# Attention scores as pairs of 64-row matmuls on the two row halves, in periods of three key-tile pairs, with the recurrence's level rounds beside probability-value batches

## The chip, the cores and the metric

One core of a Trainium2 chip. The time is that of one launch of the whole layer in device microseconds, lower is better; the median of three runs is given. TensorE (PE, with its weight loads PEld), VectorE (DVE), ScalarE (ACT) and GpSimd (POOL) work in parallel, each in the order of its own queue, and wait for one another by semaphores. SyncE (SP) issues the DMAs.

## The reference, cut to what matters

One layer of a hybrid backbone over 2048 latent and 256 context tokens, width 1024, all in 32-bit floats: a combined projection, grouped-query attention (8 query heads on 2 key heads, head size 64) beside a gated linear recurrence in both directions (4 heads of 128), an output projection and a feed-forward part. The change is in the attention; the recurrence runs between.

```python
def latent_attention(qx, kx, vx, kc, vc):
    keys = jnp.concatenate([kc, kx], axis=1)          # 2304 keys
    vals = jnp.concatenate([vc, vx], axis=1)
    scale = ATT_HEAD_DIM ** -0.5
    def block(q):                                     # 128 queries
        s = jnp.einsum('bqkgd,bnkd->bkgqn', q, keys).astype(jnp.float32) * scale
        p = jax.nn.softmax(s, axis=-1)
        return jnp.einsum('bkgqn,bnkd->bqkgd', p.astype(vals.dtype), vals)
```

## The kernel before

After the projections, one stage does attention and recurrence together. Attention is cut into 32 items: a key head `g` and 128 queries `qt` of its four query heads. Queries and keys are each split into a high and a low part, so that a product of two splits needs three terms (high by high, low by high, high by low).

For an item, `chunk` (nine of them, L910 to L943) first multiplies the high parts alone, queries by 512 keys at a time for two heads, and VectorE takes the minimum of the (negated) scores over the keys. The two matmuls of a chunk use 64 rows each, one on the upper half of the array's rows and one on the lower; they write the two banks of one PSUM tile `mx`, of which there is one. `maxima` (L945) transposes the four columns `neg` and copies them with four small DMAs into row 0 of the query tile `qb`. The chunks of item n+1 are made while item n has its scores.

`scores(k)` (L954) makes one tile of 128 keys by 512 queries with two matmuls of 128 rows: `KS` holds high and low keys one above the other and meets the high queries twice; `KB` holds a row of -1 (which subtracts the maximum), zeros and the high keys, and meets `qb` with the maxima in row 0 and the low queries below. Three PSUM tiles `s` go round. ScalarE turns each into probabilities with an exponential, two tiles to one buffer `p` (a pair). POOL adds two of three pairs (`ps`, L972). `products` (L974) multiplies six key tiles' probabilities by the values, in two column halves of 64 (`av`, L981), and sums them with a column of ones in 32-column pieces (L989). `finish` (L998) spreads the reciprocal (`pb`, L1002) and scales.

The recurrence, four heads of sixteen units in all, runs in rounds of two "lanes": a round's matmuls `pa` (L646) have 128 rows and 64 columns, and the `level` behind it works on all other engines. Other steps are `diagonal` (`pd`), `keys` (`pk`), `forward` (`psf`), `backward` (`psb`) and `output` (`po`), all with 128 rows and 128 columns. A unit's start copies on ScalarE and multiplies on POOL.

TensorE's order in this stage is written out by hand: 18 ticks to an item, one score tile to a tick; `CHUNKS` gives the ticks of the chunks, `LAGT` puts a batch of products three ticks behind its scores, and a round of the recurrence comes every ninth tick. So some rounds fall beside a batch and others between scores. The other engines' orders are the framework's, from the order in which the work is written.

Of the kernel before, what the change touches and what calls it, by code (L numbers as in the profile page):

```python
# [9 lines left out]
F32 = mybir.dt.float32  # L10
F32R = mybir.dt.float32r
# [57 lines left out]
def block_kernel(ctx: ExitStack, tc: tile.TileContext, a: dict, out: bass.AP, dbg=None):  # L69
# [141 lines left out]
    with ExitStack() as st:  # L211
# [217 lines left out]
        def qk_side(t, c):  # L429
# [55 lines left out]
            else:  # L485
# [11 lines left out]
                for g in range(2):  # L497
                    nc.sync.dma_start(s_k[g][:, t * P:(t + 1) * P], f32v(sf[:, g * P:(g + 1) * P]))
# [69 lines left out]
    with ExitStack() as st:  # L568
# [327 lines left out]
        BATCH = 6  # L896
        LAGT = 3

        class Item:
# [7 lines left out]
            def load(self):  # L907
                self.qa = qpl.tile([P, 512], F32R, tag="qa", name=f"qa{self.nm}", bufs=3)
                src = s_q[self.g][self.qt]
                for dup in range(2):  # L910
                    nc.sync.dma_start(f32v(self.qa[dup * 64:(dup + 1) * 64, :]),
                                      src[0].rearrange("d h x -> d (h x)"))

            def load_low(self):
                self.qb = QB[self.n % 2]
                nc.sync.dma_start(f32v(self.qb[64:, :]), s_q[self.g][self.qt, 1].rearrange("d h x -> d (h x)"))

            def chunk(self, c):

                if c == 0:  # L920
                    self.mn = sm.tile([P, 4, 5], F32, tag="mn", name=f"mn{self.nm}")
                s = ps_mx.tile([P, 2, 512], F32, tag="x", name=f"mx{self.nm}_{c}")
                if self.n in (NCH, NCH + 1):
                    sides = ((slice(0, P), KS[self.g]),) * 2
                else:
                    sides = ((slice(0, 64), KS[self.g]), (slice(64, P), KB))

                def part(o, h0, k0, n):
                    for i, (ps, K) in enumerate(sides):
                        nc.tensor.matmul(s[:, i, o:o + n], self.qa[ps, (h0 + i) * P:(h0 + i + 1) * P],  # L930
                                         K[ps, k0:k0 + n], start=True, stop=True)

                if c < 8:
                    h, k = c // 4 * 2, c % 4
                    part(0, h, k * 512, 512)
                    nc.vector.tensor_reduce(self.mn[:, h:h + 2, k], s, axis=AX.X, op=ALU.min)  # L936
                else:
                    for h in range(0, 4, 2):
                        part(h * 128, h, 2048, 256)
                    nc.vector.tensor_reduce(self.mn[:, :, 4].rearrange("p (h i) -> p i h", i=2),  # L940
                                            s.rearrange("p i (h k) -> p i h k", h=2), axis=AX.X, op=ALU.min)
# [3 lines left out]
            def maxima(self):  # L945

                pm = ps_h.tile([P, 512], F32, tag="h", name=f"pn{self.nm}")
# [3 lines left out]
                for h in range(4):  # L951
                    nc.sync.dma_start(f32v(self.qb[0:1, h * P:(h + 1) * P]), f32v(mr[h:h + 1, :]))

            def scores(self, k):  # L954

                nm = f"{self.nm}_{k}"
                p = k // 2
                if k % 2 == 0:
                    self.pairs[p] = pp.tile([P, 1024], F32, tag="p", name=f"p{self.nm}_{p}")
                s = ps_st.tile([P, 512], F32, tag="s", name=f"s{nm}")  # L960
                ks = slice(k * P, (k + 1) * P)
                nc.tensor.matmul(s, KS[self.g][:, ks], self.qa, start=True, stop=False)  # L962
                nc.tensor.matmul(s, KB[:, ks], self.qb, start=False, stop=True)  # L963
                o = k % 2 * 512
                nc.scalar.activation(self.pairs[p][:, o:o + 512], s, AF.Exp, scale=-1.0)  # L965
                if k % BATCH == 3:
                    self.add(p)
# [641 lines left out]
```

## Time and profile before

| what | us |
|---|---|
| median of 3 runs (3406.96 to 3409.92) | 3408.22 |
| the profiled execution's own time | 3398.26 |
| its span, first to last instruction | 3396.5 |
| stage with scores, first to last (L962) | 755.8 to 1839.2 |
| items in the stage | 32 |

The profiled execution is a little faster than the median of the runs; durations come from it. In a row of the timeline stand start, length, engine, line, operation, output and inputs with their shape, and in brackets how long the engine was idle ahead and who released it. A matmul's length includes its way through the array; the distance between two starts tells what it costs in a stream. A group's row gives count, busy time, mean in ns and idle time ahead.

### The profile page before, as it was taken

What the parts mean: (1) busy time and instruction counts of PE and PEld (TensorE: products, weight loads), DVE (VectorE), ACT (ScalarE), POOL (GpSimd) and SP (SyncE); (2) the same over time, 40 slices, a digit from 0 to 9 for tenths busy, and PEclk for the clock granted to TensorE, in tenths of its full rate; (3) what the DMA queues carried; (4) which work ended last, traced back from release to release, by engine and by line L of the source; (5) the groups of instructions that cost most, each with busy time, mean ns of one, the idle gap of its engine ahead of it and who ended that gap; (6) DMA issues with size and microseconds to landing.
All of it is one profiled execution on the core that took longest, in us unless ns stands there. A gap on an engine that the chain in (4) does not pass through costs nothing. (4 is left out here: it accounts for less than half of the span.)

```text
span 3396.5 us, 55490 instructions
## 1 busy us (share of the span) xinstructions
PE 3235.6 (95%) x21212; PEld 2514.5 (74%) x21212; DVE 1725.5 (51%) x2742; ACT 1303.6 (38%) x2559; POOL 1636.5 (48%) x1450
## 2 busy tenths in 40 slices
PE   7999999979999999999999999999989989999998
PEld 5998977965666666656667887788868768888887
DVE  6344555224555455555553557444465743333566
ACT  4322222214444444444443224333344443333444
POOL 4322223105666666666644218776631357666222
PEclk9999999989999999999999999999989999999999
DMA  7243445341111111201105444444475543323754
GB/s 238 86 150 125 136 143 150 94 135 35 29 34 43 52 39 42 63 28 46 31 16 157 132 142 131 154 152 158 159 253 188 187 128 103 100 95 103 255 197 161
DMA packets 364459, 396.75 MB, mean 117 GB/s; under 512 B 30848, under 2 KB 261216, under 8 KB 363808
## 3 DMA queue, kind: packets, MB, share of 16 engines
q1 hardware_dynamic: 364192, 393.20, 36.2%
q8 instruction: 166, 2.72, 0.3%
q14 instruction: 101, 0.83, 0.1%
HBM read 271.90 MB, written 121.13 MB: 116 GB/s over the span
## 5 line engine op out<-in xcount | busy, mean ns | idle before, releaser
L936 DVE TENSOR_REDUCE mn<-mx 128x2 f32<-128x1024 f32 x256 | 313.2, 1223 | 418.8 <-PE mx L930 322.3
L965 ACT ACTIVATE p<-s 128x512 f32<-128x512 f32 x576 | 326.8, 596 | 469.8 <-PE s L963 467.9
L972 POOL TENSOR_TENSOR ps<-p,p 128x1024 f32<-128x1024 f32 x96 | 228.4, 2379 | 276.7 <-ACT p L965 276.5
L962 PE MATMUL s<-qa,K 128*128 128x512 f32 x576 | 271.3, 471 | 0.0
L981 PE MATMUL av<-p,VS 128*64 128x256 f32 x2304 | 270.6, 384 | 0.0
L963 PE MATMUL s<-qb,KB 128*128 128x512 f32 x576 | 232.5, 404 | 4.0 <-DMA KB<-s_k 3.2
L981 PEld LDWEIGHTS av<-p,VS 128*64 128x64 f32 x2304 | 158.1, 138 | 86.8 <-issue 15.7
L1500 POOL TENSOR_TENSOR y<-y,yg 128x512 f32<-128x512 f32 x48 | 76.1, 1600 | 284.1 <-DVE yg L1499 280.3
L930 PE MATMUL mx<-K,qa 64*128 64x512 f32 (+3 forms) x340 | 151.5, 470 | 63.3 <-DVE mn L936 63.2
L930 PEld LDWEIGHTS mx<-K,qa 64*128 64x128 f32 (+1 forms) x340 | 61.1, 190 | 163.9 <-DVE mn L936 127.7
L962 PEld LDWEIGHTS s<-qa,K 128*128 128x128 f32 x576 | 109.9, 191 | 71.1 <-issue 41.5
L1469 DVE TENSOR_TENSOR x<-lr,x 128x512 fp32r<-128x512 f32 x154 | 119.8, 813 | 67.2 <-ACT x L1468 64.5
L1469 DVE TENSOR_TENSOR dl<-lr,dh 128x512 fp32r<-128x512 f32 x154 | 118.6, 809 | 64.9 <-ACT dh L1468 64.8
L930 PE MATMUL mx<-KB,qa 64*128 64x512 f32 x300 | 138.9, 479 | 0.0
L1468 ACT ACTIVATE dh<-lr 128x512 fp32r<-128x512 f32 x154 | 89.4, 623 | 109.0 <-PE pd1A L1523 51.8
L343 PE MATMUL f<-hTh,wh 128*128 128x512 f32 (+1 forms) x320 | 122.4, 382 | 7.4 <-ACT ft L372 7.4
L1468 ACT ACTIVATE x<-lr 128x512 fp32r<-128x512 f32 x154 | 90.5, 626 | 93.8 <-PE pd0A L1523 38.5
L1330 PE MATMUL pA<-x,A11h 128*128 128x512 f32 x352 | 113.7, 403 | 9.7 <-ACT A11h L1303 7.4
L963 PEld LDWEIGHTS s<-qb,KB 128*128 128x128 f32 x576 | 111.2, 193 | 13.6 <-DMA KB<-s_k 3.5
L1523 PE MATMUL pd0A<-x,x 128*128 128x512 f32 x528 | 120.7, 389 | 0.0
L343 PE MATMUL f<-hTh,wl 128*128 128x512 f32 (+1 forms) x320 | 119.8, 375 | 0.0
L343 PE MATMUL f<-hTl,wh 128*128 128x512 f32 (+1 forms) x320 | 119.7, 374 | 0.0
(345 smaller groups left out, 9238.1 us busy)
## 6 DMA issues: line engine op xcount, KB each, us to landing
w<-in_w_gu_dram SPq DMA_DIRECT2D x88, 512.0 KB
wm<-in_w_mod_dram SPq DMA_DIRECT2D x24, 1024.0 KB
lr<-s_wT SPq DMA_DIRECT2D x88, 256.0 KB
lr<-in_w_down_dram SPq DMA_DIRECT2D x66, 256.0 KB
wq<-in_w_down_dram SPq DMA_DIRECT2D x44, 256.0 KB
s_wT<-wq SPq DMA_DIRECT2D x44, 256.0 KB
lr<-s_hid1S SPq DMA_DIRECT2D x44, 256.0 KB
lr<-s_hid0S SPq DMA_DIRECT2D x44, 256.0 KB
```

Source lines behind the costliest of these rows:

```text
L343: nc.tensor.matmul(pm[:, :n], w[wi][:, k, c0:c0 + P], hT[b][hi][:, k, :], start=(k == 0 and i == 0), stop=(k == KT - 1 and i == 2))
L930: nc.tensor.matmul(s[:, i, o:o + n], self.qa[ps, (h0 + i) * P:(h0 + i + 1) * P], K[ps, k0:k0 + n], start=True, stop=True)
L936: nc.vector.tensor_reduce(self.mn[:, h:h + 2, k], s, axis=AX.X, op=ALU.min)
L962: nc.tensor.matmul(s, KS[self.g][:, ks], self.qa, start=True, stop=False)
L963: nc.tensor.matmul(s, KB[:, ks], self.qb, start=False, stop=True)
L965: nc.scalar.activation(self.pairs[p][:, o:o + 512], s, AF.Exp, scale=-1.0)
L972: nc.gpsimd.tensor_tensor(t, self.pairs[p - 1], self.pairs[p], op=ALU.add)
L981: nc.tensor.matmul(self.av[i * 64:(i + 1) * 64, :256], VS[:, k, self.g * 64:(self.g + 1) * 64], self.pairs[k // 2][:, o:o + 256], start=(k ...
L1330: nc.tensor.matmul(acc, w[wi][:, k, :], x[xi][k], start=(start and k == 0 and i == 0), stop=(stop and k == KH - 1 and i == 2), skip_group_ ...
L1468: nc.scalar.activation(hi, src, AF.Copy)
L1469: nc.vector.tensor_tensor(lo, src, f32v(hi), op=ALU.subtract)
L1523: nc.tensor.matmul(cur[t], l[:, t * P:(t + 1) * P], r, start=(start and j == 0 and f == 0), stop=(stop and j == NHF - 1 and f == 2), skip_ ...
```

## The change

All scores are made with 64 rows. Keys are laid out in two halves: even key tiles in the upper 64 partitions and odd ones in the lower, high parts in `KH` and low parts in `KL`, both groups loaded at the start. `scores(p)` makes a pair of key tiles at once, with four matmuls for each half (high by high, low by high, high by low, and the maxima through `KM` and `qm`), the halves alternating. The queries stand twice, once in each half. The maxima are copied with eight DMAs, four for each half. A chunk has 384 keys for each half of one head, there are twelve, and the minimum runs over both banks.

The 18 ticks become three periods (`NPER`) of three pairs (`GP`). A period `b` is: chunk, pair 3b+1, chunk, pair 3b+2, chunk, the next period's first pair, chunk, batch of products. The recurrence's steps go into four places of a period (`STEPS`), and both rounds of an item into the last place of the second and third period, straight ahead of a batch. Reading out the products (`drain`) moves behind the next item's first chunk.

```diff
+                    o = t % 2 * (NTOK // 2) + t // 2 * P
+                    nc.sync.dma_start(s_k[g][:, o:o + P], f32v(sf[:, g * P:(g + 1) * P]))
...
             def chunk(self, c):
+                h, k = divmod(c, 3)
+                for i in range(2):
+                    rw = slice(i * 64, (i + 1) * 64)
+                    nc.tensor.matmul(s[:, i, :384], self.qa[rw, h * P:(h + 1) * P],
+                                     KH[self.g][rw, k * 384:(k + 1) * 384], start=True, stop=True)
+                nc.vector.tensor_reduce(self.mn[:, h, k:k + 1], s[:, :, :384], axis=AX.XY, op=ALU.min)
...
-                for h in range(4):
-                    nc.sync.dma_start(f32v(self.qb[0:1, h * P:(h + 1) * P]), f32v(mr[h:h + 1, :]))
...
-                nc.tensor.matmul(s, KS[self.g][:, ks], self.qa, start=True, stop=False)
-                nc.tensor.matmul(s, KB[:, ks], self.qb, start=False, stop=True)
...
+                for i in range(2):
+                    for h in range(4):
+                        nc.sync.dma_start(f32v(self.qm[i * 64:i * 64 + 1, h * P:(h + 1) * P]), f32v(mr[h:h + 1, :]))
...
+                s = [ps_st.tile([P, 512], F32, tag="s", name=f"s{self.nm}_{p}{i}") for i in range(2)]
+                hi, lo = (K[self.g][:, p * P:(p + 1) * P] for K in (KH, KL))
+                ops = (hi, self.qa), (lo, self.qa), (hi, self.qb), (KM, self.qm)
+                for f, (k, q) in enumerate(ops):
+                    for i in range(2):
+                        rw = slice(i * 64, (i + 1) * 64)
+                        nc.tensor.matmul(s[i], k[rw, :], q[rw, :], start=(f == 0), stop=(f == 3))
+                for i in range(2):
+                    nc.scalar.activation(t[:, i * 512:(i + 1) * 512], s[i], AF.Exp, scale=-1.0)
+                if p % GP == 1:
                     self.add(p)
...
-        CHUNKS = (-3, -1, 0, 2, 3, 5, 7, 9, 11)
...
+        STEPS = [[(0, 0)], [(0, 1)], [], [(0, 2)], [(0, 3)], [(0, 4)], [], [(0, 5)],
+                 [(1, 0), (1, 1)], [(1, 2)], [(1, 3)], [(1, 4), (1, 5)]]
...
+                chunk(4 * x)
+                if b == 0 and n:
+                    items[n - 1].drain()
+                item.scores(GP * b + 1)
+                rest(0)
+                chunk(4 * x + 1)
+                rest(1)
+                item.scores(GP * b + 2)
+                if b == 0 and n:
+                    items[n - 1].finish(ps_h, "h")
+                chunk(4 * x + 2)
+                rest(2)
+                if x + 1 < NPER * NIT:
+                    items[(x + 1) // NPER].scores((x + 1) % NPER * GP)
+                made = rest(3)
+                if b == 1 and n + 1 < NIT:
+                    items[n + 1].maxima()
+                chunk(4 * x + 3)
+                next(made, 0)
+                item.products(b)
+                next(made, 0)
```

TensorE between two score tiles in the middle of an item, before. The names are the output, then the stationary and the moving tile as the row has them.

```order
L962 MATMUL s_0_9_9983<-qa_0_9337,K_7774 128x512
L963 MATMUL s_0_9_9983<-qb_7778,KB 128x512
L930 MATMUL mx_0_7_9989<-K_7774,qa_0_9687 128x512
L930 MATMUL mx_0_7_9989<-KB,qa_0_9687 128x512
L962 MATMUL s_0_10_9994<-qa_0_9337,K_7774 128x512
L963 MATMUL s_0_10_9994<-qb_7778,KB 128x512
```

The same place with the change: one pair between two chunks.

```order
L930 MATMUL mx_0_1_11256<-Kh_7774,qa_0_10968 128x384 x2
L957 MATMUL s_0_70_11261<-qa_0_10193,Kh_7774 128x512
L957 MATMUL s_0_71_11262<-qa_0_10193,Kh_7774 128x512
L957 MATMUL s_0_70_11261<-qa_0_10193,Kl_7776 128x512
L957 MATMUL s_0_71_11262<-qa_0_10193,Kl_7776 128x512
L957 MATMUL s_0_70_11261<-qb_0_10570,Kh_7774 128x512
L957 MATMUL s_0_71_11262<-qb_0_10570,Kh_7774 128x512
L957 MATMUL s_0_70_11261<-qm_7780,KM 128x512
L957 MATMUL s_0_71_11262<-qm_7780,KM 128x512
L930 MATMUL mx_0_2_11295<-Kh_7774,qa_0_10968 128x384 x2
```

A chunk of two matmuls, then eight matmuls where four stood for the same two tiles; chunk and scores now have the same number of rows.

TensorE at a level round, before: this round stands between a chunk and a score tile, away from the products.

```order
L930 MATMUL mx_0_1_10083<-K_7774,qa_0_10015 128x512
L930 MATMUL mx_0_1_10083<-KB,qa_0_10015 128x512
L646 MATMUL pa_10087<-Q_9131,M_5_9962 64x64 x8
L646 MATMUL pa_10087<-Q_9665,M_2_9973 64x64 x8
L962 MATMUL s_0_0_10131<-qa_0_9687,K_7774 128x512
L963 MATMUL s_0_0_10131<-qb_7779,KB 128x512
```

With the change, the same kind of round, with the maxima's transpose ahead of it.

```order
L957 MATMUL s_0_61_11161<-qm_7780,KM 128x512
L941 MATMUL pn_0_11172<-identr,neg_0_11157 4x128
L930 MATMUL mx_0_0_11185<-Kh_7774,qa_0_10968 128x384 x2
L647 MATMUL pa_11189<-Q_10852,M_1_10947 64x64 x8
L647 MATMUL pa_11189<-Q_10077,M_5_10958 64x64 x8
L977 MATMUL av_0_11072<-p_0_3_11038,VS 64x256 x4
```

The round goes straight into the products, which have the same shape of 128 rows by 64 columns; the transpose stands between two pieces of 64-row work.

SyncE around an item's maxima, before:

```order
L952 DMA qb_7779<-mr_0_10029 1x16x8 x4
L911 DMA qa_0_10358<-s_q_72 64x512
L916 DMA qb_7778<-s_q_72 64x512
L911 DMA qa_0_10358<-s_q_72 64x512
L1005 DMA s_att_77<-oo_0_10211 128x2x128
```

and with the change:

```order
L946 DMA qm_7781<-mr_0_10361 1x16x8 x8
L919 DMA qa_0_10567<-s_q_72 64x512 x2
L919 DMA qb_0_10570<-s_q_72 64x512 x2
L1002 DMA s_att_77<-oo_0_10620 128x2x128
L946 DMA qm_7780<-mr_0_10730 1x16x8 x8
```

Thirteen issues to an item where eight stood, in the same sequence.

More of the change, by code (lines that the diff above doesn't have):

```diff
@@ L1055, in block_kernel, with rest @@
[L1055 to L1059 removed]
+        for x in range(-5, 0):
+            chunk(x)
+        items[0].scores(0)
+        for x in range(NPER * NIT + 1):
+            n, b = divmod(x, NPER)
+            item = items[n] if n < NIT else None
+            def rest(i, item=item, n=n, b=b):
+                made = iter(())
+                for hr, j in STEPS[b * 4 + i]:
+                    hr += 2 * n
+                    if j == 0:
+                        rec.begin(hr)
+                    rec.step(hr, j)
+                    if j != 5:
+                        next(rec.beside, 0)
+                    else:
+                        made = rec.round()
+                return made
+            if item is not None:
+                if b == 0 and n + 2 < NIT:
+                    items[n + 2].load()
+                if b == 0 and n + 1 < NIT:
+                    items[n + 1].load_low()
+                chunk(4 * x)
[19 more added lines that the diff above has]
+                next(made, 0)
```

164 lines of the change are left out of this document (58 added, 106 removed).

## Prediction

> **What bounds the kernel now.** I read the page's busy line and its 40 slices first, then the windows by stage, then the waits, and last TensorE's timeline over one item of the attention stage.
>
> ```profile
> PE 3235.6 (95%) x21212; PEld 2514.5 (74%) x21212; DVE 1725.5 (51%) x2742; ACT 1303.6 (38%) x2559; POOL 1636.5 (48%) x1450
> L962 PE MATMUL s<-qa,K x576: 387/496/794, 755.8 to 1839.2; 128*128 128x512 f32 x192
> 1200.00:1400.00 200.00, 185.56 (x1861) 128.47 (x1859) 108.96 (x164) 91.53 (x195) 130.19 (x145) 0.99 0.17 48
> ```
>
> Columns of the window row: length, then busy time of PE, PEld, DVE, ACT, POOL, granted clock, DMA share, GB/s. The change touches the stage from 755.8 to 1839.2 us (32 items, 1083 us) and the 29 us before it. TensorE is busy 93% of the window, the clock is full, the other engines have a third to a half of it free. So a stage time is TensorE's own time plus what it waits, and its own time holds more than streams:
>
> ```profile
> 1202.41 0.71 PE L1002 MATMUL pb<-li,pick 128*128 128x128 f32 x4
> 1205.07 1.19 PE L646 MATMUL pa<-Q,M 128*64 128x64 f32 x32
> 1206.09 2.76 PE L981 MATMUL av<-p,VS 128*64 128x256 f32 x24
> 1208.78 0.64 PE L989 MATMUL av<-ps,one 128*32 128x128 f32 x16
> 1209.79 0.50 PE L962 MATMUL s<-qa,K 128*128 128x512 f32 x1
> 1210.13 0.40 PE L963 MATMUL s<-qb,KB 128*128 128x512 f32 x1
> 1210.45 0.49 PE L930 MATMUL mx<-K,qa 64*128 64x512 f32 x1
> 1210.46 0.49 PE L930 MATMUL mx<-KB,qa 64*128 64x512 f32 x1
> 1210.88 0.50 PE L962 MATMUL s<-qa,K 128*128 128x512 f32 x1
> 1211.22 0.40 PE L963 MATMUL s<-qb,KB 128*128 128x512 f32 x1
> 1211.46 0.40 PE L962 MATMUL s<-qa,K 128*128 128x512 f32 x1
> 1211.69 0.40 PE L963 MATMUL s<-qb,KB 128*128 128x512 f32 x1
> 1212.28 0.39 PE L930 MATMUL mx<-K,qa 64*128 64x256 f32 x1 [0.18 <-DVE mn L936]
> 1232.06 0.71 PE L1002 MATMUL pb<-li,pick 128*128 128x128 f32 x4
> 1446.39 0.71 PE L1002 MATMUL pb<-li,pick 128*128 128x128 f32 x4
> ```
>
> Three readings. A 512-column stream among its like takes 0.23 us (1211.22 to 1211.46 to 1211.69). A visit of the 64-row chunk among 128-row scores changes the array's shape twice: from 1210.13 to 1211.46 there are four streams, 0.93 us, in 1.33 us, so a visit costs 0.40 and one change 0.20; 0.11 of it is the first stream's weights, which cannot be loaded ahead (0.34 instead of 0.23 after the change). And an item without other recurrence work than its two level rounds takes 29.65 us (1202.41 to 1232.06), while seven items in a row, one head of the recurrence, average (1446.39 - 1202.41) / 7 = 34.85.
>
> ```profile
> PE mx L930 <- DVE mn L936: 43.4, 91, 3.6
> PEld mx L930 <- DVE mn L936: 99.5, 134, 4.1
> 1210.99 1.23 DVE L936 TENSOR_REDUCE mn<-mx 128x2 f32<-128x1024 f32 x1 [3.32 <-PE mx L930]
> 1210.56 0.60 ACT L965 ACTIVATE p<-s 128x512 f32<-128x512 f32 x1 [2.96 <-PE s L963]
> 1200.83 1.08 ACT L965 ACTIVATE p<-s 128x512 f32<-128x512 f32 x2 [0.16 <-PE s L963]
> ```
>
> The wait that TensorE has now is for the chunk's two-bank tile: matmul at 1210.45, minimum from 1210.99 to 1212.22, next matmul at 1212.28. Scores wait for nobody: each exponential (0.60 us, 0.54 in a run) follows its score tile 0.43 us after the last stream's start, and three score tiles go round.
>
> **The change part by part.** *Array shapes.* I counted changes of shape in TensorE's order (rows by columns of each line): 847 before, 613 after. At 0.20 each that is 47 us less on TensorE, all of it in the stage. What stands against it are new waits, so I lay out one period of the new order from the rows above, with 0 at the first chunk's weight load.
>
> *Streams.* A pair's scores are four streams on each half. If the halves run at once, the pair costs 4 x 0.232 = 0.93, just as two 128-row tiles cost now. That weights go in under the stream in this shape too is seen in one place:
>
> ```profile
> 1000.76 0.38 PE L930 MATMUL mx<-K,qa 64*128 64x256 f32 x1
> 1000.87 0.19 PEld L930 LDWEIGHTS mx<-K,qa 64*128 64x128 f32 x1
> 1000.98 0.28 PE L930 MATMUL mx<-K,qa 64*128 64x256 f32 x1
> ```
>
> The first stream (0.11 us of weights, then 0.11 of columns) runs from 1000.87, and the next weights of the same half start just then; the second matmul streams at once (0.28 against 0.38 long).
>
> *Chunks.* 12 of 384 columns for 9 of 512: 12 x 0.17 = 2.1 us, as 9 x 0.23 was. The minimum shrinks:
>
> ```profile
> L936 DVE TENSOR_REDUCE mn<-mx 128x2 f32<-128x1024 f32 x245 | 299.7, 1223 | 316.8 <-PE mx L930 315.2
> L760 DVE TENSOR_REDUCE sso<-o 128x4 f32<-128x512 f32 x16 | 10.8, 678 | 17.2 <-ACT o L758 17.2
> L994 DVE RECIPROCAL li<-av 128x128 f32<-128x128 f32 x31 | 29.6, 955 | 53.6 <-PE av L989 53.6
> L1004 DVE TENSOR_TENSOR oo<-ot,pb 128x256 f32<-128x256 f32 x31 | 12.7, 410 | 0.0
> ```
>
> From 678 ns for 512 elements and 1223 for 1024, 768 take about 0.95; chunk to chunk 0.48 + 0.95 + 0.06 = 1.49 at least.
>
> *One period.* Chunk 0: weights to 0.11, stream to 0.28. Pair A streams 0.28 to 1.21; both its tiles end together, so its exponentials run only then, 1.41 to 2.01 and 2.01 to 2.55. Chunk 1 may start at 1.49 (0.28 waited), stream to 1.77. Pair B: the first half takes the third score tile at once, the second half needs the tile that A's first exponential frees: 2.01 + 0.06 + 0.11 = 2.18, end 3.11 instead of 2.70. Chunk 2 to 3.28. Pair C's second half waits for B's first exponential (3.19 to 3.79): 3.96, end 4.89 instead of 4.21. Chunk 3 to 5.06, change of shape 0.10, probability-value batch 2.69 (1206.09 to 1208.78), sums 1.01 (1208.78 to 1209.79): 8.86 us. Of this 0.28 + 0.41 + 0.68 = 1.4 us is waiting, of a kind that the kernel does not have now. An item: 3 x 8.86, two level rounds at 1.02 (1205.07 to 1206.09), 0.6 in the first period where reciprocal (0.96) and product (0.41) push the minima on VectorE, 0.4 for the maxima's transpose between 64-row work: 29.6 us against 29.65. **Nothing gained in a plain item**: the drains saved (about 2 us) and the chunk waits saved (1.7 us) are paid back as 4.3 us of waits for exponentials.
>
> *Recurrence work between.* It stays 128 rows deep and now stands in a 64-row stream. In one head's seven items the order has 25 such places, two changes each, 10 us. In return such a place fills a wait: before chunk 1 up to 0.7, before B 0.4, before C 0.7, before chunk 3 nothing; by the places counted, also about 10 us. I enter zero. The remaining 34.85 - 29.65 = 5.2 us an item (work and VectorE waits) I leave as it is.
>
> *Order on ACT.* At a head's start (four times) the context unit's copies stand ahead of pair A's exponentials, some of them behind POOL's products; before, single score tiles had three buffers of slack there, now the second half of B waits. I take 2 us each, 8 us (bounds 0 and 5 each).
>
> *Start and middle.*
>
> ```profile
> 748.22 0.79 PE L930 MATMUL mx<-K,qa 64*128 64x512 f32 x1 [1.32 <-DVE mn L936]
> 750.33 0.58 PE L930 MATMUL mx<-K,qa 64*128 64x256 f32 x1 [1.32 <-DVE mn L936]
> 755.83 0.79 PE L962 MATMUL s<-qa,K 128*128 128x512 f32 x1
> 753.40 2.49 SPq L952 DMA_DIRECT2D qb<-mr  x4
> 757.16 0.77 PE L963 MATMUL s<-qb,KB 128*128 128x512 f32 x1 [0.54 <-DMA qb<-mr]
> PE s L963 <- DMA KB<-s_k: 3.2, 1, 3.2
> ```
>
> Ahead of the first scores chunks run alone, 2.11 us apart at the low clock (748.22 to 750.33), about 1.75 in the new size. Twelve and then five stand there instead of nine and two; part of the five is work that no longer stands between scores. I take +4 us. The maxima's eight copies issue in 5 us where four took 2.49 and land about 1.3 later; within an item they have 9 us (a level round, a batch, two pairs), so they stay hidden, with 2 us to spare. Reloading the low-key tile at the group's change goes: -3.2.
>
> **Sum**: 0 + 0 + 8 + 4 - 3 = +9 us. The profiled execution took 3398.26 us, 10 below the median of the runs, 3408.22; the same step on the median gives **3417 us**.
>
> **The rivals.** *The drains win.* The extra 5.2 us an item in busy items hold 3.6 of matmul work and 1.6 of waits, most behind 1.22 us minima; with 0.95 ones and recurrence work filling the exponential waits these may go: 31 x 1.6 = 50 us, 3367 us. For it: 143 us of chunk waits in the rows above. Against it: the recurrence's own VectorE work is unchanged and still goes ahead of the minima.
>
> *Exponentials late.* The second half of the next pair starts only when ScalarE has done one exponential, so any other ScalarE work ahead of it is now on the path; before, it was not. In the stage that work is:
>
> ```profile
> L672 ACT ACTIVATE C<-C 128x256 f32<-128x256 f32 (+1 forms) x139 | 55.6, 400 | 21.5 <-POOL C L668 9.2 <-POOL kk L625 8.1
> L671 ACT ACTIVATE M<-C 128x256 f32<-128x256 f32 (+1 forms) x139 | 55.1, 397 | 36.4 <-PE pa L646 15.5 <-POOL M L665 13.9 <-POOL C L668 5.4
> L616 ACT ACTIVATE M<-F 128x512 f32<-128x512 f32 (+1 forms) x19 | 12.0, 633 | 12.2 <-DMA F<-s_f 6.3 <-PE pa L646 3.6 <-POOL M L665 1.7
> ```
>
> 111 us of level copies and some 60 of others (12 such as the last row, and keys, diagonals, squares), plus their own waits. If 60 to 70 us of it falls between A's scores and C's, the time is 3480. It decides where copies stand between two pairs rather than under the batch; the level rounds beside the batch speak against it.
>
> *Loads not hidden.* If weights of a half cannot go in while that half streams, each of 288 pairs pays 4 x 0.11: 127 us, 3545. The rows at 1000.87 speak against it, though they show two streams and not eight. The Trainium skill ("TensorE: Matmul & The Clock Gate", Part 3, The mechanism) says that weight loads overlap matmuls in flight only when their row group differs, which would be this case; the loads at 1000.87 started with the stream of their own row group, and the 128-row loads are hidden too, so the trace does not agree.
>
> **How the numbers follow.** Forecast 0.45, within 3395 to 3440; drains win 0.23; exponentials late 0.25; loads 0.07. Of the forecast's own range about a quarter is faster by over 0.2% (below 3401.4; 0.2%, 7 us, is about what a measurement tells from no change), a quarter within it, half slower. Faster 0.11 + 0.23 = 0.34; same 0.12; slower 0.22 + 0.25 + 0.07 = 0.54. The range takes in the drains' rival and the late exponentials: 3360 to 3482, leaving out the loads and the tails.
>
> **What would show it.** Right: a plain item of 29 to 30 us between two pb rows; TensorE idle for exponentials, about 1 us a period, where now it is idle for minima; pairs of 0.93 us; no wait for the maxima's copies. Wrong: pairs of 1.3 us or more (loads); second halves that do not wait (drains win); items above 31 us with level copies between pairs (exponentials late).

## The result, and the profile after

The change makes the kernel slower: 3420.97 us against 3399.20 for the kernel before, medians of 11 runs each (3416.30 to 3427.93, and 3392.04 to 3411.95). The ratio is 1.0062, with a 95% interval from 1.0045 to 1.0078, so about 21 us where 9 were forecast. The profiled execution of the changed kernel is the longest of its eleven: 3427.93 us, span 3426.1.

The first view is the page's busy line and the group of the minimum; the second is a window of the attention stage, with the columns that the prediction explained.

```profile
PE 3263.6 (95%) x22492; PEld 2554.9 (75%) x22492; DVE 1743.9 (51%) x2838; ACT 1300.3 (38%) x2559; POOL 1636.4 (48%) x1451
...
L932 DVE TENSOR_REDUCE mn<-mx 128x1 f32<-128x768 f32 x384 | 366.7, 955 | 462.3 <-PE mx L930 460.4
```

```profile
1200.00:1400.00 200.00, 188.39 (x2031) 130.16 (x2031) 109.30 (x170) 92.60 (x200) 129.72 (x144) 0.97 0.15 42
```

TensorE is busy for 188.4 of 200 us where it was 185.6, so it stands idle less, and yet the stage is longer. The number that got worse is the third from the right: the granted clock, 0.97 for 0.99.

Where the 29.6 us between the two profiled spans lie, from the first start of each piece of work on TensorE (us from the start of the span; "pb" is the product that ends an item, there are 32):

| | before | after | stretch ending here, difference |
|---|---|---|---|
| first chunk | 727.2 | 733.3 | +6.1 |
| first pb | 799.85 | 804.95 | -1.0 |
| 31st pb (30 items later) | 1823.11 | 1842.33 | +14.1 |
| last matmul of the output projection | 2035.8 | 2064.5 | +9.5 |
| end of the span | 3396.5 | 3426.1 | +0.9 |

The first row is chance: over the fourteen kernels profiled in this study the first chunk starts between 719.8 and 733.3, in either order of the work. The rest, 23.5 us, agrees with the medians. It lies in the 30 items and in the stretch behind the 31st.

A period in an item with little other work shows whether the layout held (TensorE's timeline):

```profile
1747.80 0.44 PE L930 MATMUL mx<-Kh,qa 64*128 64x384 f32 x2
1748.08 0.40 PE L957 MATMUL s<-qa,Kh 64*128 64x512 f32 x2
1748.31 0.39 PE L957 MATMUL s<-qa,Kl 64*128 64x512 f32 x2
...
1749.30 0.44 PE L930 MATMUL mx<-Kh,qa 64*128 64x384 f32 x2
1749.58 0.76 PE L957 MATMUL s<-qa,Kh 64*128 64x512 f32 x2
1749.84 0.72 PE L957 MATMUL s<-qa,Kl 64*128 64x512 f32 x2
...
1750.80 0.44 PE L930 MATMUL mx<-Kh,qa 64*128 64x384 f32 x2
1751.07 0.92 PE L957 MATMUL s<-qa,Kh 64*128 64x512 f32 x2
...
1752.62 0.27 PE L941 MATMUL pn<-identr,neg 128*4 128x128 f32 x1
1752.82 0.44 PE L930 MATMUL mx<-Kh,qa 64*128 64x384 f32 x2
1753.19 1.15 PE L647 MATMUL pa<-Q,M 128*64 128x64 f32 x32
1754.18 2.76 PE L977 MATMUL av<-p,VS 128*64 128x256 f32 x24
...
1757.88 0.44 PE L930 MATMUL mx<-Kh,qa 64*128 64x384 f32 x2
```

The two halves stream at once ("x2", the next pair of streams 0.23 us later). From chunk to chunk there are 10.08 us; without the maxima's transpose (0.20) and the level round (0.99) that stand in this period, 8.89, where 8.86 were laid out. Chunks start 1.50 us apart. The rows of 0.76 and 0.92 us are pairs whose second half starts late: one half streams alone while the other waits for an exponential, and since TensorE streams, this wait is not idle time. The whole item, from the pb at 1741.53 to the one at 1770.96, takes 29.43 us; 29.6 were forecast.

So plain items came out as laid out. The items with recurrence work did not. The lengths of seven items in a row, in us, from pb to pb (one head of the recurrence):

```
before 1202.41 on: 29.6 34.8 37.9 39.7 37.1 32.2 32.6
after  1213.49 on: 34.2 34.1 34.3 43.4 34.7 38.0 31.0
```

The first of them is the item that the prediction measured as plain: 29.65 us before, 34.2 after. It is read through here, on TensorE, VectorE, POOL and SyncE in turn (the timeline, from the pb at 1213.49):

```profile
1213.49 0.71 PE L999 MATMUL pb<-li,pick 128*128 128x128 f32 x4
1216.57 0.44 PE L930 MATMUL mx<-Kh,qa 64*128 64x384 f32 x2 [2.37 <-DVE mn L932]
...
1217.86 1.82 PE L705 MATMUL psf<-V,kt 128*128 128x128 f32 x8
...
1220.23 3.46 PE L977 MATMUL av<-p,VS 128*64 128x256 f32 x24
...
1214.43 1.22 DVE L684 TENSOR_REDUCE T<-F 128x512 f32<-128x1024 f32 x1 [1.81 <-DMA F<-s_f]
1215.57 0.95 DVE L932 TENSOR_REDUCE mn<-mx 128x1 f32<-128x768 f32 x1
...
1209.06 1.00 POOL L680 TENSOR_TENSOR Q<-Q,F 128x256 f32<-128x256 f32 x1
...
1210.08 0.33 SPq L606 DMA_DIRECT2D F<-s_f  x1
```

Read from the bottom: POOL's product, F's last reader, ends at 1210.06, the load of the next unit's F is issued at 1210.08 and used at 1214.43. VectorE's reduction of F stands ahead of the chunk's minimum in its queue, waits 1.81 us and runs 1.22, and only then the minimum frees the tile that the next chunk needs. TensorE is idle for 2.37 us. What follows is the surprise: `psf` takes 1.82 us and the batch 3.46, where the same rows take 1.16 and 2.81 elsewhere. The windows of those microseconds give the granted clock (third number from the right):

```profile
1215.00:1217.00 2.00, 0.43 (x4) 0.43 (x6) 1.84 (x3) 0.00 (x0) 2.00 (x2) 1.00 0.01 4
1217.00:1219.00 2.00, 2.00 (x16) 1.56 (x13) 0.96 (x1) 1.04 (x2) 2.00 (x2) 0.79 0.21 66
1219.00:1221.00 2.00, 2.00 (x10) 1.20 (x10) 1.00 (x2) 0.05 (x1) 0.40 (x1) 0.50 0.00 0
1221.00:1223.00 2.00, 2.00 (x18) 1.22 (x16) 1.26 (x4) 0.00 (x0) 0.00 (x0) 0.86 0.00 0
```

After the gap the clock is halved for some 3.4 us, which loses 0.42 + 1.00 + 0.28 = 1.7 us of work. Such stretches of 3.4 or 6.8 us add up to 23.9 us in the 30 items before and to 47.8 after (TensorE's clock record in the trace, stretch by stretch). This gives the account on which the experiments are read. For the 30 items: idle time (the waits in brackets in TensorE's rows, summed), half of the time at half clock, and the rest, which is work at full clock:

| 30 items, us | length | idle | at half clock | rest |
|---|---|---|---|---|
| before | 1023.3 | 54.8 | 23.9 | 956.5 |
| after | 1037.4 | 41.5 | 47.8 | 972.0 |
| difference in the length | +14.1 | -13.3 | +12.0 (half of 23.9) | +15.5 |

Each row comes from one execution. That the changed kernel gets the lower clock holds for all of them: over the whole launch it is 0.976 to 0.978 in its eleven executions, and 0.979 to 0.984 in those of the kernel before that ran beside the experiments. The idle time is also put together in another way: 103 waits before, 8 of them of 1.4 us or more; 40 waits after, 12 of them of 1.4 us or more.

### The profile page after: what moved, and what is told of

Same layout as the page of the kernel before. It is cut to its first block, busy times and chain, and to the rows that moved or that the text cites. A ratio compares the mean times of both kernels' runs of the same rounds, so it can differ in the third digit from the quotient of the medians.

```text
span 3426.1 us, 58424 instructions
## 1 busy us (share of the span) xinstructions
PE 3263.6 (95%) x22492; PEld 2554.9 (75%) x22492; DVE 1743.9 (51%) x2838; ACT 1300.3 (38%) x2559; POOL 1636.4 (48%) x1451
## 5 line engine op out<-in xcount | busy, mean ns | idle before, releaser
L932 DVE TENSOR_REDUCE mn<-mx 128x1 f32<-128x768 f32 x384 | 366.7, 955 | 462.3 <-PE mx L930 460.4
L959 ACT ACTIVATE p<-s 128x512 f32<-128x512 f32 x576 | 312.4, 594 | 418.2 <-PE s L957 417.2
L930 PE MATMUL mx<-Kh,qa 64*128 64x384 f32 x768 | 176.9, 442 | 59.0 <-DVE mn L932 49.4
L930 PEld LDWEIGHTS mx<-Kh,qa 64*128 64x128 f32 x768 | 76.8, 190 | 143.8 <-DVE mn L932 108.2
L957 PE MATMUL s<-qa,Kh 64*128 64x512 f32 x576 | 169.8, 437 | 8.4 <-ACT p L959 7.2
L957 PE MATMUL s<-qa,Kl 64*128 64x512 f32 x576 | 154.4, 421 | 0.0
L957 PE MATMUL s<-qb,Kh 64*128 64x512 f32 x576 | 142.6, 401 | 0.0
L957 PE MATMUL s<-qm,KM 64*128 64x512 f32 x576 | 142.4, 400 | 0.0
L1540 PEld LDWEIGHTS pd0A<-x,x 128*128 128x128 f32 x528 | 99.1, 188 | 20.6
```

The source lines that it names most:

```text
L930: nc.tensor.matmul(s[:, i, :384], self.qa[rw, h * P:(h + 1) * P], KH[self.g][rw, k * 384:(k + 1) * 384], start=True, stop=True)
L932: nc.vector.tensor_reduce(self.mn[:, h, k:k + 1], s[:, :, :384], axis=AX.XY, op=ALU.min)
L957: nc.tensor.matmul(s[i], k[rw, :], q[rw, :], start=(f == 0), stop=(f == 3))
L959: nc.scalar.activation(t[:, i * 512:(i + 1) * 512], s[i], AF.Exp, scale=-1.0)
L1540: nc.tensor.matmul(cur[t], l[:, t * P:(t + 1) * P], r, start=(start and j == 0 and f == 0), stop=(stop and j == NHF - 1 and f == 2), skip_ ...
```

## The experiments

All ratios are to the kernel before, measured beside it, with 95% intervals. "Items" is the length of the 30 items as above.

**Halved exponentials, in both kernels.** The edit, in the changed kernel (in the kernel before it is the same on its single tile; the lines by which the batch and POOL's sum read the kept half twice are left out here):

```
-nc.scalar.activation(t[:, i * 512:(i + 1) * 512], s[i], AF.Exp, scale=-1.0)
+nc.scalar.activation(t[:, i * 512:i * 512 + 256], s[i][:, :256], AF.Exp, scale=-1.0)
```

> The changed kernel with only 256 of each score tile's 512 columns put through the exponential (the batch reads those twice; the other half is left out). Theory A, the prediction's (second halves wait for ScalarE's exponentials): an exponential of 0.54-0.60 us falls to about 0.35, B's second half then waits 0.2 instead of 0.41 and C's 0.3 instead of 0.68, 0.6 us a period, 96 periods, so about 55 us less than the changed kernel (ratio to before 0.990, 0.986 to 0.995). Theory B, the price of the new order is TensorE at half clock after gaps that VectorE's queue makes, and the exponentials' waits only stand where others would: less than 15 us (ratio 1.002 to 1.006).

> The kernel before with the same halved exponentials. Both theories: score tiles had three buffers of slack, so no change, ratio 0.998 to 1.002. If it falls as much as the changed kernel does, ScalarE's other waits are shortened in both and the experiment on the changed kernel does not speak for its exponential waits.

Measured: 1.0071 (1.0057 to 1.0085) for the changed kernel, 1.0005 (0.9991 to 1.0019) for the one before, which does not change, as both theories had it. The changed kernel gains nothing (1.0062 with whole exponentials), so Theory A falls, but not because the waits for exponentials stayed. In the table of the weight loads' waits (us in total, times, longest) they go from 43.7 to 9.6; first the changed kernel, then the one with halved exponentials:

```profile
PEld mx L930 <- DVE mn L932: 81.3, 119, 3.8
PEld s L957 <- ACT p L959: 43.7, 110, 1.3
```

```profile
PEld mx L930 <- DVE mn L932: 96.9, 129, 4.1
...
PEld s L957 <- ACT p L959: 9.6, 18, 1.2
```

The rest falls by 15.7 us, to 956.3, the value of the kernel before: that was the price of halves that stand while the other half streams (in the kernel before the same edit leaves the rest as it is, 956.1). Idle time takes 10.0 of it back (the chunk's tile is the next limit: chunks still start 1.49 us apart, and a plain item is only 0.3 to 0.5 us shorter), and the stretches at half clock grow from 47.8 to 68.3 us. The items take 1042.0 us, 4.6 more than with whole exponentials.

**All chunks 128 rows deep, before.**

```
-if self.n in (NCH, NCH + 1):
+if True:
     sides = ((slice(0, P), KS[self.g]),) * 2
```

> The kernel before with every chunk's matmuls 128 rows deep (as it has them for two items): no change of array rows round a chunk, but its two matmuls no longer run at once. At 0.20 us a change: nine visits an item, 0.40 each, 3.6 us less; 9 x 0.23 = 2.1 us more of streams; 29 items x -1.5 = -45 us, some of it taken back by the chunk-to-chunk interval growing by 0.23: ratio 0.987 to 0.995. Rival, the changes cost nothing that the wait for VectorE's minima would not: +2.1 x 29 = +60 us, ratio 1.010 to 1.018.

Measured: 1.0041 (1.0027 to 1.0055), between the two. Its timeline shows both answers:

```profile
1776.98 0.39 PE L963 MATMUL s<-qb,KB 128*128 128x512 f32 x1
1777.21 0.62 PE L930 MATMUL mx<-K,qa 128*128 128x512 f32 x2
1777.68 0.40 PE L962 MATMUL s<-qa,K 128*128 128x512 f32 x1
1777.91 0.39 PE L963 MATMUL s<-qb,KB 128*128 128x512 f32 x1
...
1779.16 0.73 PE L930 MATMUL mx<-K,qa 128*128 128x256 f32 x4 [0.40 <-DVE mn L936]
```

Where TensorE does not wait, four streams take 0.93 us with a chunk among them and nothing for a change of shape; the prediction's price of 0.40 a visit is right there, and a visit is 0.17 cheaper (0.23 for the second stream). Where the chunk waits for VectorE, the change of shape lay inside the wait and saves nothing, and the second stream costs its 0.23. The kernel before has 134 waiting visits of about 270 by its wait table: -0.17 x 136 + 0.23 x 134 = +8 us by this estimate; the items show +15, so half of it is left unexplained.

**Two buffers for F, in both kernels.** In the one before, the states `Sb` go from eight buffers to six to make room.

```
-self.F = up.tile([P, 512, 2], F32, tag="F", name=f"F{h}{u}", bufs=1)
+self.F = up.tile([P, 512, 2], F32, tag="F", name=f"F{h}{u}", bufs=2)
```

> The changed kernel with two buffers for the recurrence's F tile, so that its load no longer waits for POOL's products on the one before, and VectorE's reduction T<-F no longer stands waiting ahead of a chunk's minimum. Theory B (gaps of 1.3 to 3.3 us at a unit's start, behind most of them TensorE at half clock for 3.4 or 6.8 us): 16 units x (about 1.5 us of gap + 1.5 us of lost clock) = 30 to 50 us less, granted clock in the stage back to 0.99, ratio to before 0.992 to 0.999. Theory A (gaps at unit starts are the same in both kernels and only pass to the next wait): within 10 us of the changed kernel, ratio 1.003 to 1.008.

> The kernel before with two buffers for F (and six instead of eight for the readout's states Sb, to make room). Theory B1, a unit's F load costs both kernels alike: its gaps of 3.64, 2.54, 2.37 and 2.54 us for the minimum go, with the half clock behind them, ratio 0.990 to 0.996. Theory B2, in the order before the reduction T<-F mostly falls where TensorE has a batch or scores to run, so that only the new order pays for it: within 6 us, ratio 0.998 to 1.002.

Measured: 0.9998 (0.9988 to 1.0009) for the changed kernel, so 22 us less than without, and 0.9967 (0.9954 to 0.9979) for the one before, 11 us less. Theory B has the mechanism for the changed kernel, but not the size: 22 us lie below its 30 to 50. The profiled items take 1005.5, with idle 28.4, half clock 15.6, rest 969.3. Of the 32 us by which these two executions differ in the items, 13 are idle time, 16 lost clock and 3 the rest. The order before gains half as much, so it lies between B1 and B2; in its items (1018.0, 5.3 less) the gain is in clock (13.7 us at half clock instead of 23.9), hardly in idle time (54.0 for 54.8). This is also the version that beats both kernels: the order before with two F buffers, 10 to 11 us faster than the kernel before. With F out of the way the new order is 12.5 us shorter than the old in the 30 items (1005.5 against 1018.0) and still 0.3% slower as a whole.

**Three buffers for F.** `bufs=3` in the same line of the changed kernel.

> The changed kernel with three buffers for F. With two, a gap of 2.5 to 3.3 us stays at each of the four head starts, where three units (two lanes and the context) want an F at once, followed each time by 3.4 or 6.8 us of half clock. If the gaps are F's buffers: 4 x (2.8 + 2.5) = 20 us less than with two buffers, ratio to before 0.992 to 0.996. If something else is late there (POOL's queue, the load itself): within 5 us of two buffers, 0.998 to 1.001.

Measured: 1.0022 (1.0010 to 1.0035), 8 us more than with two, outside what either theory allowed. The gaps at the head starts stay and have a new name (TensorE, then ScalarE, then POOL):

```profile
1262.88 0.38 PE L957 MATMUL s<-qa,Kh 64*128 64x512 f32 x1
1266.64 0.79 PE L957 MATMUL s<-qa,Kh 64*128 64x512 f32 x1 [3.37 <-ACT p L959]
...
1264.05 0.32 ACT L673 ACTIVATE C<-C 128x128 f32<-128x128 f32 x1 [6.04 <-POOL C L669]
...
1259.07 2.55 POOL L628 TENSOR_TENSOR Q<-q,F 128x512 f32<-128x512 f32 x2 [3.95 <-DMA q<-s_hq]
```

A level's copy C<-C, of the context unit (128 columns in a half, where the other units have 256), stands ahead of the exponentials that this half waits for, and itself waits 6.04 us for POOL. POOL is late because it now has the next unit's products ahead of the context's, and these wait 3.95 us for the load of `q`, a tile that still has one buffer; with two buffers for F the context's product came first (1252.99 us in that trace, the next unit's at 1256.71). The same wait for `q` stands at the other two head starts within the items (3.69 and 4.51 us). So the third buffer moved the stall to the next single buffer; whether a second one for `q` would end it is not tested.

**Work put into the gaps.** First twelve matmuls ahead of each of nine chunks:

```
+FILL = {13, 35, 74, 97, 158, 181, 227, 242, 265}
 def chunk(x):
+    if x in FILL:
+        av = items[x // 12 - (x % 12 < 4)].av
+        for _ in range(12):
+            nc.tensor.matmul(av[:, 384:512], pick[:, 0, :], ident, start=False, stop=False, skip_group_check=True)
```

> The changed kernel, one F buffer, with twelve useless 128x128 matmuls (1.3 us, into columns of the av tile that nobody reads) on TensorE ahead of each of nine chunks, those at which its profile shows gaps of 1.4 to 3.3 us for the minimum, 19.5 us in all, and behind them 41 us at half clock. Theory C, the idle gap itself halves the clock and half of the stretch is lost: work put into the gap costs nothing and most of the 41 us run at full clock, 10 to 20 us less than the changed kernel, ratio to before 1.000 to 1.003. Rival, the clock falls for another reason (VectorE's or ScalarE's burst, a budget over a longer time): nothing gained, the matmuls cost up to 4 us where they outlast a gap, ratio 1.005 to 1.008.

Measured: 1.0091 (1.0074 to 1.0107), slower, even more than the rival had it, but not for the rival's reason. The filler was twice as long as reckoned (each of these float matmuls shows as two rows), and at four of the nine places it did not run in the gap: it waited for the reciprocal, which reads the same tile.

```profile
1279.94 4.56 PE L1036 MATMUL av<-identr,pick 128*128 128x128 f32 x24 [3.22 <-DVE li L993]
...
1215.29 2.84 PE L1036 MATMUL av<-identr,pick 128*128 128x128 f32 x24
...
1219.36 1.16 PE L705 MATMUL psf<-V,kt 128*128 128x128 f32 x8
```

That makes it a better test than it was meant to be. At the five places where the filler filled the gap (as at 1215.29) the stretch at half clock is gone, and the `psf` behind it is back to 1.16 us. At the four where TensorE stayed idle (as at 1279.94) it is still there. Then only at those five places, with half of the filler (`FILL = {35, 74, 158, 227, 242}`, `range(6)`):

> The changed kernel with useless matmuls only at the five places where those of the run before ran inside the gap, and half as many, 1.4 us each, shorter than each of the gaps (1.69, 1.69, 1.69, 2.37 and 2.62 us in the changed kernel). Theory C, an idle gap halves the clock: the five stretches of 3.4 us at half clock (at 862, 968, 1217, 1422 and 1466 us) go, the time to the next pb falls by 1 to 1.7 us at each, 5 to 8 us in all, ratio to before 1.0035 to 1.005. Rival, the clock costs nothing or falls anyway: the gaps stay as long or longer, ratio 1.006 to 1.008 and the five items as long as before.

Measured: 1.0054 (1.0038 to 1.0070), between the two theories; by the whole time alone this is not told from the changed kernel. The five items tell more: they are 1.76, 1.54, 2.29, 1.84 and 1.64 us shorter, 9.1 in all, though TensorE does 1.5 us of useless work in each, and none of the five places has a stretch at half clock. (All 30 items take 1027.1, with 23.4 us at half clock for 47.8; 17.1 of this difference are the five stretches, the rest lies at places without filler, where the stretches differ too.) The place read through above, now:

```profile
1199.65 0.71 PE L999 MATMUL pb<-li,pick 128*128 128x128 f32 x4
1200.20 1.50 PE L1036 MATMUL av<-identr,pick 128*128 128x128 f32 x12
1202.02 0.44 PE L930 MATMUL mx<-Kh,qa 64*128 64x384 f32 x2 [0.32 <-DVE mn L932]
...
1203.31 1.16 PE L705 MATMUL psf<-V,kt 128*128 128x128 f32 x8
...
1204.77 2.81 PE L977 MATMUL av<-p,VS 128*64 128x256 f32 x24
```

The chunk starts 2.37 us behind the pb's row instead of 3.08, and from there to the batch it takes 2.75 us instead of 3.66. The first difference is not the clock's: in this execution VectorE had its F 3.65 us after the load's issue, for 4.35 above. Over the five places quicker loads make up about 1.1 of the 9.1 us; the other 8 are near what five stretches lose, 1.7 us each.

**Where the level rounds stand.** In the changed kernel the second round moves to between the last period's second chunk and third pair; in the kernel before, the second round alone is put beside a batch:

```
-[(1, 0), (1, 1)], [(1, 2)], [(1, 3)], [(1, 4), (1, 5)]]
+[(1, 0), (1, 1)], [(1, 2), (1, 3), (1, 4), (1, 5)], [], []]
...
-rest(1)
+made = rest(1)
+next(made, 0)
+next(made, 0)
```
```
-STEPS = {0: 0, 1: 1, 3: 2, 4: 3, 6: 4, 7: 5}
+STEPS = {0: 0, 1: 1, 3: 2, 4: 3, 6: 4, 7: 5, 9: 0, 10: 1, 11: 2, 12: 3, 13: 4, 14: 5}
...
-if x % 9 == 8:
+if x % 18 in (8, 14):
```

> The changed kernel with an item's second level round moved from beside the last batch to between the last period's second chunk and its third pair; one F buffer, as changed. If a round among 64-row work costs two changes of shape and its copies on ScalarE delay exponentials that the next pair waits for: 0.4 to 1.5 us for each of 32 rounds that exist, 13 to 45 us more than the changed kernel, ratio 1.009 to 1.020. If it only fills a wait that is there anyway: within 6 us, ratio 1.004 to 1.008.

> The kernel before with this part of the change alone: the second level round of an item stands beside the batch at its tile 14 instead of among scores at tile 17, its six steps at tiles 9 to 14. At 0.20 us a change of shape, one or two changes less an item, 6 to 12 us less: ratio 0.9965 to 0.998. Rival: the recurrence's steps bunched in six tiles make VectorE's queue later for the minima: ratio 1.001 to 1.006.

Measured: 1.0249 (1.0229 to 1.0268), about 60 us more than the changed kernel and more than the expectation allowed, and 1.0082 (1.0070 to 1.0094), where 6 to 12 us of gain were expected. In the first the place reads like this on TensorE, then on ScalarE (one timeline):

```profile
1152.64 0.39 PE L957 MATMUL s<-qa,Kh 64*128 64x512 f32 x1
1155.73 0.50 PE L957 MATMUL s<-qa,Kh 64*128 64x512 f32 x1 [2.70 <-ACT p L959]
...
1151.14 0.69 ACT L617 ACTIVATE M<-F 128x512 f32<-128x512 f32 x1 [3.28 <-PE pa L647]
1151.72 0.44 ACT L672 ACTIVATE M<-C 128x256 f32<-128x256 f32 x1
1154.77 0.42 ACT L673 ACTIVATE C<-C 128x256 f32<-128x256 f32 x1 [2.62 <-POOL kk L626]
1155.10 1.07 ACT L959 ACTIVATE p<-s 128x512 f32<-128x512 f32 x2
```

The level's copies, one of them waiting 2.62 us for POOL, stand ahead of the exponentials. That is the mechanism of the prediction's rival "exponentials late". The edit moves the round between two pairs and also puts four steps into one place; which of the two makes the copies late it does not separate. The items take 1100.4 us: idle 77.6 (22.5 of it for exponentials, 6.1 in the changed kernel), half clock 109.7, rest 967.9. In the second the rest falls as was reckoned for the shapes (949.0, 7.5 less than before), but idle time grows by 21.8 us and half clock by 27.3. Its rival's sign was right, with more than its size.

**Rounds evenly spaced.** The item's twelve places with one step each, rounds at the sixth and the twelfth, with two F buffers (and the round called behind a period's second chunk, as above):

```
-STEPS = [[(0, 0)], [(0, 1)], [], [(0, 2)], [(0, 3)], [(0, 4)], [], [(0, 5)],
-         [(1, 0), (1, 1)], [(1, 2)], [(1, 3)], [(1, 4), (1, 5)]]
+STEPS = [[(0, 0)], [(0, 1)], [(0, 2)], [(0, 3)], [(0, 4)], [(0, 5)], [(1, 0)], [(1, 1)],
+         [(1, 2)], [(1, 3)], [(1, 4)], [(1, 5)]]
```

> The changed kernel with two buffers for F and the item's two level rounds 6 and 6 of its 12 places apart instead of 4 and 8: the first round moves from beside the second batch to between that period's second chunk and its third pair, the steps one to a place. Theory S, what made the moved rounds dear (28 us in the order before, 56 more in the new one) is that a level's work on POOL, VectorE and ScalarE, some 10 us, has a third or less of an item until its next round: evenly spaced that wait goes, 10 to 25 us less than with two buffers alone, though the round costs two changes of shape, ratio to before 0.993 to 0.998. Theory X, a round between pairs is dear because its copies stand ahead of exponentials: 13 to 45 us more, ratio 1.004 to 1.013.

Measured: 1.0028 (1.0015 to 1.0040), 10 us more than with two buffers alone. Theory S falls: rest and idle time in the items are nearly the same (970.0 and 29.5 for 969.3 and 28.4), and what grows is the time at half clock, from 15.6 to 32.1 us. The same idle time is in longer pieces: three new gaps of 1.9 us for an item's joined minimum (`neg`, L935), each followed by 3.4 or 6.8 us at half clock. Theory X is not needed either: a round stands between two pairs here, and the plain items stay at 31.2 us for 31.0. What exactly makes `b_rounds` idle more stays open.

**The end of the stage.**

```
-[(0, 5), (1, 0), (1, 1), (1, 2), (1, 3), (2, 0), (2, 1), (2, 2)]
+[(0, 5), (1, 0), (1, 1), (1, 2), (1, 3), (1, 4), (1, 5), (2, 0)]
```

> The changed kernel with two buffers for F and the last head's last three readout steps set earlier (the last output in the first place of the last item instead of the third). The first weight load of the output projection, which takes the recurrence's memory, was issued 3.3 us ahead of the product pb of the last but one item before the change and 3.7 us behind it after. If this lateness is what makes the time from that pb to the end 10 us longer (1573.4 to 1583.7 us), 5 to 9 us go: ratio to before 0.996 to 0.9985, and that stretch 1574 to 1579. If the ten come from the last item's own order, the ratio stays at 0.999 to 1.001.

Measured: 0.9986 (0.9975 to 0.9997), not told from two F buffers alone. The stretch from the 31st pb to the last matmul of the projection falls from 221.9 to 216.2 us, but the 30 items grow from 1005.5 to 1010.5, 4.5 of it in the last of them, which takes the moved steps. Most of what left the one stretch came back in the other. What the changed kernel loses there can be read from its own timeline:

```profile
1844.09 0.49 PE L755 MATMUL po<-V,A 128*128 128x128 f32 x2
...
1854.93 0.74 PE L1136 MATMUL mt<-identr,mix 128*128 128x128 f32 x3 [1.14 <-DMA mix<-s_hg]
...
1857.62 0.66 PE L1136 MATMUL mt<-identr,mix 128*128 128x128 f32 x2 [1.27 <-DMA mix<-s_hg]
...
1860.21 4.31 PE L977 MATMUL av<-p,VS 128*64 128x256 f32 x24
```

The last output (2.9 us, up to 1846.96) now stands behind the 31st pb; TensorE waits 2.4 us for the mixed rows, whose transposes stand in the middle of the last item's scores; and behind that a batch runs in 4.31 us instead of 2.81, with 6.8 us at half clock (3.4 lost). That is 8.7 of the 9.5 us.

## Why the prediction was right in sign and short in size

**Streams, chunks, the period: right.** Pairs of 64-row halves take 0.93 us, so the rival on weight loads falls. The minimum takes 955 ns for an estimated 0.95, chunks start 1.50 us apart for 1.49, the period takes 8.89 us for 8.86 and the plain item 29.43 for 29.6. No row shows TensorE waiting for the maxima's copies.

**Array shapes: the price right, the gain not to be had.** 0.20 us a change holds where TensorE is not waiting. But half of the visits in the kernel before waited for a minimum anyway, and there, as `b_wide` indicates, the change of shape lay inside the wait. The 47 us never stood on the path as a whole; the layout of a period had already given nothing for them, which is why the sum was not hurt.

**Recurrence work, entered at zero: the step that failed, by what it left out.** The step set 10 us of shape changes against 10 us of filled waits in one head's seven items. In the account the 30 items have +15.5 us of rest against -13.3 of idle time: about 2 in sum, so the zero held for work and waits together, though not for its reason: the rest did not grow by shapes, and halving the exponentials, which ends the standing of halves, takes 15.7 of it away. What was missing stands two parts earlier in the prediction, where the clock of the window, 0.99, was read as "full", and where a busy item's remaining 5.2 us were left as they were. The clock is not a constant: behind most of the gaps of 1.4 us or more (11 of 13 here, 7 of 9 in the kernel before) it is halved for 3.4 us or more, so that such a gap costs its own length and then 1.7 us or more again. The waits got fewer in total, but at the units' starts they fell in the first period of an item, behind one chunk tile, and eleven of them brought a stretch at half clock where seven had. That is the +12.0 us. The five filled gaps show that the gap brings the stretch, and two buffers for F that most of these gaps are F's.

**Order on ScalarE, +8: right in sum, wrong in kind.** The head-start items did grow by about 4 us (39.7 to 43.4), but with two F buffers they take 40.5. Here it was the F gap and the clock, not the context's copies. The mechanism that the prediction named is real all the same: with three F buffers the context's copy stands ahead of a pair's exponentials and TensorE waits 3.37 us for it.

**Start, +4: it is -1.** The five chunks that now stand ahead of the first scores come off the first item entirely. **Reload, -3.2:** gone as said; it is part of the idle time that fell.

**The end of the stage, not in the sum: +9.5.** The prediction counted what the change moves within items and did not ask what the last item hands on to the output projection.

**What was luck.** Of the two terms that made the sum positive, the start came out at -1 and the order on ScalarE had another cause; what made the kernel slower, the clock and the end of the stage, was not in the sum. So the sign came right only in part by the prediction's working. That the measured 3421 lies so near to the forecast 3417 is luck as well: the kernel before came out 9 us below the median that the forecast was added to (3399.20 for 3408.22), and the change cost 12 us more.

**The rivals.** Drains did not win. The 143 us of chunk waits held up for them is more than there was: it adds TensorE's idle time (43.4) to that of its weight loads (99.5), which overlap. Exponentials were not late in the changed kernel, where TensorE idles 6.1 us for them; `a_roundmid` shows that this rival was real. The prediction let the place between two pairs decide, and that is not the whole of it: with the steps spread evenly a round stands there too, and TensorE idles 8.5 us for exponentials, for 4.9 with two F buffers alone. The waits for exponentials cost 15.7 us of rest and still were not worth removing by themselves.

## What to carry to other kernels

Sum the idle time, the time at half clock and the rest of a stage separately; a change that lowers the idle time can still lose when it turns many short waits into a few gaps of 2 us. Before a reordering, look for a load with one buffer whose consumer stands in an in-order queue ahead of work that the bottleneck waits for: here a second buffer for F was worth 11 us in the old order, where the whole reordering brought nothing, with one buffer or with two. Then look which single buffer is next: a third one for F only moved the stall to `q`. A saving that lies under a wait is no saving; count it only for the visits that do not wait.

## What the runs showed of the hardware

Gaps far shorter than the stretch of half clock that follows are enough. In the changed kernel, from 800 to 1845 us, TensorE has 13 gaps of 1.4 us or more; behind 11 of them the granted clock is 0.50 for 3.4 or 6.8 us, down to gaps of 1.43 and 1.69 us. None follows the three gaps of 1.05 to 1.27 us. The Trainium skill ("TensorE: Matmul & The Clock Gate", the section "Why this matters for your kernels") warns of idle gaps above about 3 us between bursts; the rows here show the fall after about half of that.

Two gaps of 1.92 and 2.38 us have no such stretch behind them, so length alone does not decide. Where a gap falls matters too: in the clock records of all fourteen kernels every change of the clock lies on a fixed grid of 3.413 us, to within 6 ns, whatever the kernel does. The gap of 2.38 us lies astride a point of this grid, with 1.35 us ahead of it and 1.03 behind; so do two in `a_fill6`, of 2.30 (1.45 and 0.85) and 2.43 us (1.50 and 0.94), which have none either, while at the same two places of the changed kernel gaps of 2.26 and 2.42 us lie between two points and 6.8 us at half clock follow each. The grid does not settle every case: the gap of 1.92 us lies between two points and has none, and one of 2.46 us lies astride a point and has one. A stretch more or less in a single trace can therefore be chance.

Useless matmuls in such a gap pay for themselves. With 1.5 us of them in a gap of 1.7 to 2.6 us the item was 1.5 to 2.3 us shorter, up to 0.7 of it by a quicker load, and at none of the ten places filled in `a_fill` and `a_fill6` did a stretch at half clock follow.
